# Where sixteen DRAM-to-DRAM copies of the window cache stand in SyncE's queue, in a two-layer hybrid decoder step

## The chip, the cores and the metric

The kernel runs on one core of a Trainium2 chip. The metric is device time in microseconds (us) of one execution; lower is better. Times of the kernel before are three timed runs and their median; the trace comes from one further execution under the hardware profiler.

## What is computed

One inference step of a decoder, two layers deep, for a prompt of 512 tokens and 8 sample sequences of one token each. Every layer normalizes its input, multiplies by `w_in`, runs a convolution branch and a sparse-attention branch, multiplies by `w_out`, normalizes and adds the residual. Beside the two activations the step returns updated caches. One of them is the point here: the window cache of the samples, 512 rows of keys and values per sequence, shifted up by one row with the new token's row put last.

```
win_rows = jnp.stack([kw, vw], axis=2)
win_ext = jnp.concatenate([pad_rows, win_buf, win_rows], axis=1)
win_new = win_ext[:, win_ext.shape[1] - n_keep:]
```

So for each layer and each of 8 sequences 511 of 512 old rows are copied from the input `cache_win` to the output one row higher: 16 copies of 1022 KB, from DRAM to DRAM. Nothing in the kernel reads them again.

## The kernel before

Each layer runs through four stages. `phase_a1` multiplies the normalized input by most of `w_in`, while the generator `compress` gathers pages of the cache (tile `G`, GpSimd), transposes them (tile `T`, VectorE), splits each into a high and a low part (`th`, `tl`) and multiplies by the compression weights (`w1f`, split into `w1h` and `w1l`). `phase_a2` does the rest of `w_in` and the attention of the samples. `phase_b` does the attention of the prompt, head by head, with column blocks of the `w_out` product as filler. `phase_c` finishes the `w_out` product and, in layer 0, starts the compression of layer 1.

A matrix product (`gemm`) loads 512 KB of weights into `wf` (two buffers, line 332), splits them into `wh` (ScalarE, line 374) and `wl` (VectorE or GpSimd, line 375), and multiplies three times per tile: `wh` by the high part of the input (350), `wh` by the low part (351), `wl` by the high part (352), into PSUM tile `g`.

In `phase_b`, `heads()` goes over four key/value heads. Each loads its keys twice into `kk` (one tile for the selected, one for the window branch, line 1436; split into `kh` and `kl`) and its values into `vnat`, and then over four query heads: a head loads its rotated query into `qq` (three buffers, two DMAs, line 1456), makes `qs` of it, and runs `stage1` (scores, softmax in `smx`) and `stage2` (transposes, product with values into `po`) for both branches. After every second head the gate `zt` (one buffer) is loaded and multiplied in on GpSimd (1422). Ahead of the heads stands the softmax of the compressed blocks, tile `sct`, whose exponential is line 1305.

All plain DMAs are issued by SyncE (SP), in the order of its program; indirect gathers are issued by GpSimd. The order of each engine's program is not the order of the Python code: a scheduler simulates the kernel when it is built and lets each engine take, by priority, what its simulation finds ready. Loads of weights are marked high priority. A copy of the window cache reads only an input and writes only an output, so it is ready at any moment. `tc.issue_after(ins)` adds an order edge: what the block issues on that engine stands behind `ins` in its program.

Of the kernel before, what the change touches and what calls it, by code (L numbers as in the profile page):

```python
# [372 lines left out]
def split(g, dst_h, dst_l, src, eng=None):  # L373
    g.nc.scalar.activation(dst_h, src, AF.Copy)  # L374
    return (eng or g.nc.vector).tensor_tensor(dst_l, src, dst_h.bitcast(F32), op=ALU.subtract)  # L375
# [382 lines left out]
def shift_window(g, l, s):  # L758
    n = 4 * 511
    row = 2 * NKV * HD  # L760
    at = (l * NS + s) * WIN * row
    g.nc.sync.dma_start(
        bass.AP(g.wins_o.tensor, at, [[n, 128], [1, n]]),
        bass.AP(g.a["cache_win"].tensor, at + row, [[n, 128], [1, n]]),
    )
# [498 lines left out]
def phase_b(g, l, mix):  # L1264
    nc, tc, K, ident = g.nc, g.tc, g.K, g.ident
    q_d, qr_d, kr_d, kvn_d, z_d = g.q_d[l], g.qr_d[l], g.kr_d[l], g.kvn_d[l], g.z_d[l]
    gnat = g.gnat
    with ExitStack() as sb:
# [6 lines left out]
        for kv in range(4):  # L1275
            pst = mi.tile([128, 512], F32, tag="t", bufs=PS_T, name="psc_t")
            for t2 in range(2):
                qt = pool.tile([128, SEQ], F32, tag="qq", name="qu", bufs=3)
                nc.sync.dma_start(qt, q_d[2 * kv + t2, :, 0:SEQ])
                for par in range(2):  # L1280
                    gg = 2 * t2 + par
# [147 lines left out]
        def heads():  # L1429
            units = []  # L1430
            for kv in range(4):
                kh_, kl_, vs_ = [], [], []
                for ty in range(2):
                    kk = pool.tile([128, SEQ], F32, tag="kk", name="kk")
                    for hh in range(2):
                        nc.sync.dma_start(
                            kk[64 * hh:64 * hh + 64], kr_d[2 * ty + kv // 2, 64 * (kv % 2):64 * (kv % 2) + 64, 0:SEQ]
                        )
                    kh2 = pool.tile([128, SEQ], F32R, tag=f"kh{ty}", name="kh2")
                    kl2 = pool.tile([128, SEQ], F32R, tag=f"kl{ty}", name="kl2")  # L1440
                    split(g, kh2, kl2, kk, nc.gpsimd)
                    kh_.append(kh2)
                    kl_.append(kl2)
                    vn_ = pool.tile([128, 4, 64], F32, tag="vnat", name="vnat")
                    c0 = (3 + 2 * ty) * 256 + kv * 64
                    nc.sync.dma_start(vn_, kvn_d[:, c0:c0 + 64].rearrange("(t p) f -> p t f", p=128))
                    v2 = pool.tile([128, 4, 128], F32R, tag=f"v2{ty}", name="v2")
                    split(g, v2[:, :, 0:64], v2[:, :, 64:128], vn_, nc.gpsimd)
                    vs_.append(v2)
                for s in (2 * kv, 2 * kv + 1):  # L1450
                    shift_window(g, l, s)
                for gg in range(4):
                    h = 4 * kv + gg
                    qq = pool.tile([128, SEQ], F32, tag="qq", name="qq", bufs=3)
                    for hh in range(2):
                        nc.sync.dma_start(
                            qq[64 * hh:64 * hh + 64], qr_d[h // 2, 64 * (h % 2):64 * (h % 2) + 64, 0:SEQ]
                        )
                    qs = pool.tile([128, SEQ], F32R, tag="qs", name="qs")
                    nc.scalar.activation(qs, qq, AF.Copy)  # L1460
                    nc.gpsimd.tensor_tensor(qs[64:128], qq[64:128], qs[64:128].bitcast(F32), op=ALU.subtract)
                    for ty in range(2):
                        units.append(stage1(h, ty, qs, kh_[ty], kl_[ty], vs_[ty]))
                        if len(units) > 1:
                            stage2(*units.pop(0))
            stage2(*units.pop(0))
# [9 lines left out]

        fill = gemm(g, _jobs(g.a["w_out"][l], 0, range(NPART), ks=(0, CT), width=128), mix, ev_part)
        heads()
        for _ in fill:
            pass  # L1480
# [190 lines left out]
```

## Time and profile before

| | before |
|---|---|
| timed runs | 3060.17, 3066.3, 3069.18 us |
| median | 3066.3 us |
| profiled execution: time, span | 3078.59 us, 3076.8 us |
| TensorE busy (share of the span) | 2707.9 us (88%) |
| VectorE | 2276.5 us (74%) |
| GpSimd | 1711.5 us (56%) |
| ScalarE | 1444.1 us (47%) |
| mean granted TensorE clock | 0.959 |
| bytes moved by DMA | 534.49 MB, mean 174 GB/s |

A busy share is a mean over stages with different limits; the section of rows below looks at stages. The profiled execution is 12.3 us longer than the median of the timed runs.

### The profile page before, as it was taken

What the parts mean: (1) busy time and instruction counts of PE and PEld (TensorE: products, weight loads), DVE (VectorE), ACT (ScalarE), POOL (GpSimd) and SP (SyncE); (2) the same over time, 40 slices, a digit from 0 to 9 for tenths busy, and PEclk for the clock granted to TensorE, in tenths of its full rate; (3) what the DMA queues carried; (4) which work ended last, traced back from release to release, by engine and by line L of the source; (5) the groups of instructions that cost most, each with busy time, mean ns of one, the idle gap of its engine ahead of it and who ended that gap; (6) DMA issues with size and microseconds to landing.
All of it is one profiled execution on the core that took longest, in us unless ns stands there. A gap on an engine that the chain in (4) does not pass through costs nothing. (4 is left out here: it accounts for less than half of the span.)

```text
span 3076.8 us, 53806 instructions
## 1 busy us (share of the span) xinstructions
PE 2707.9 (88%) x18984; PEld 2369.6 (77%) x18984; DVE 2276.5 (74%) x4432; ACT 1444.1 (47%) x3180; POOL 1711.5 (56%) x1610
## 2 busy tenths in 40 slices
PE   5498889989997998988988899899889899998896
PEld 4477778868786876867876688888878788887795
DVE  6479988877777643896999977897678765368746
ACT  4244344443333454785556544444333345468744
POOL 3376666655475654674656645565465565467502
PEclk8799999999998999999999999999999999999998
DMA  9876667755544645215777776675554464541154
GB/s 310 260 212 201 202 202 230 218 153 171 181 151 133 201 138 156 90 28 143 206 232 222 238 204 209 190 221 177 151 183 138 132 205 150 156 131 51 44 172 157
DMA packets 430318, 534.49 MB, mean 174 GB/s; under 512 B 68450, under 2 KB 357362, under 8 KB 429760
## 3 DMA queue, kind: packets, MB, share of 16 engines
q1 hardware_dynamic: 367328, 324.42, 35.4%
q0 software_dynamic: 62720, 206.63, 21.6%
q8 instruction: 149, 2.44, 0.3%
q14 instruction: 121, 0.99, 0.1%
HBM read 484.80 MB, written 64.75 MB: 179 GB/s over the span
## 5 line engine op out<-in xcount | busy, mean ns | idle before, releaser
L350 PE MATMUL g<-uh,wh 128*128 128x256 f32 (+1 forms) x3328 | 963.0, 292 | 74.8 <-ACT wh L374 60.1
L351 PE MATMUL g<-ul,wh 128*128 128x256 f32 (+1 forms) x3328 | 957.5, 290 | 0.0
L352 PE MATMUL g<-uh,wl 128*128 128x256 f32 (+1 forms) x3328 | 942.2, 291 | 11.3 <-DVE wl L375 11.3
L539 POOL DMA_INDIRECT G<-in_cache_kv_pages_dram,gix x512 | 543.5, 1062 | 355.0 <-DVE T L550 187.3
L350 PEld LDWEIGHTS g<-uh,wh 128*128 128x128 f32 x3328 | 644.0, 194 | 108.8 <-ACT wh L374 62.1
L375 DVE TENSOR_TENSOR wl<-wf,wh 128x512 fp32r<-128x512 f32 x565 | 429.0, 763 | 387.2 <-ACT wh L374 379.9
L1112 POOL DMA_INDIRECT G<-in_cache_kv_pages_dram,six x448 | 495.5, 1106 | 336.2 <-issue 113.9
L351 PEld LDWEIGHTS g<-ul,wh 128*128 128x128 f32 x3328 | 644.8, 194 | 22.9 <-issue 14.9
L352 PEld LDWEIGHTS g<-uh,wl 128*128 128x128 f32 x3328 | 633.6, 194 | 34.6 <-DVE wl L375 14.5
L374 ACT ACTIVATE wh<-wf 128x512 fp32r<-128x512 f32 x616 | 381.1, 625 | 462.1 <-PE g L351 250.2
L375 DVE TENSOR_TENSOR tl<-T,th 128x512 fp32r<-128x512 f32 x512 | 430.7, 861 | 98.3 <-ACT th L374 96.0
L374 ACT ACTIVATE th<-T 128x512 fp32r<-128x512 f32 x512 | 308.7, 624 | 312.4 <-DVE T L550 208.7
L550 DVE STREAM_TRANSPOSE T<-G 128x512 f32<-128x512 f32 x512 | 349.7, 695 | 22.0 <-DMA G<-in_cache_kv_pages_dram,gix 20.0
L887 DVE SCALAR_TENSOR_TENSOR c<-ap,cwt,c 128x512 f32<-128x512 f32 x480 | 339.4, 746 | 0.1
L579 PE MATMUL ca<-tl,w1h 128*128 128x512 f32 x512 | 218.5, 427 | 44.4 <-DVE tl L375 43.9
L578 PE MATMUL ca<-th,w1h 128*128 128x512 f32 x512 | 217.0, 424 | 24.0 <-ACT th L374 20.4
L375 POOL TENSOR_TENSOR w1l<-w1f,w1h 128x512 fp32r<-128x512 f32 x128 | 168.2, 1316 | 123.2 <-ACT w1h L374 96.3
L580 PE MATMUL ca<-th,w1l 128*128 128x512 f32 x512 | 209.2, 409 | 0.0
L1376 POOL TENSOR_TENSOR smx<-smx,su 128x256 f32<-128x256 f32 (+2 forms) x192 | 154.3, 830 | 84.0 <-DVE su L1370 63.6
L374 ACT ACTIVATE w1h<-w1f 128x512 fp32r<-128x512 f32 x128 | 79.5, 624 | 168.1 <-DMA w1f<-in_cmp_w_dram 85.7
L350 PE MATMUL g<-mha,wh 128*128 128x256 f32 (+1 forms) x512 | 144.7, 291 | 15.1 <-DVE zg L1513 8.3
L1368 ACT ACTIVATE smx<-smx,nm 128x128 f32<-128x128 f32 (+3 forms) x256 | 140.7, 552 | 35.9 <-DVE nm L1364 32.7
(1179 smaller groups left out, 5210.3 us busy)
## 6 DMA issues: line engine op xcount, KB each, us to landing
wf<-in_w_in_dram SPq DMA_DIRECT2D x220, 512.0 KB
wf<-in_w_out_dram SPq DMA_DIRECT2D x88, 512.0 KB
w1f<-in_cmp_w_dram SPq DMA_DIRECT2D x512, 64.0 KB
out_dram<-in_cache_win_dram SPq DMA_DIRECT2D x16, 1022.0 KB
G<-in_cache_kv_pages_dram,gix POOLq DMA_INDIRECT x512
wk<-in_cache_win_dram SPq DMA_DIRECT2D x16, 512.0 KB
qq<-qr_d SPq DMA_DIRECT2D x64, 128.0 KB
G<-in_cache_kv_pages_dram,six POOLq DMA_INDIRECT x448
```

Of the source, the lines that this page charges most:

```text
L350: nc.tensor.matmul(ps[m][h], lh, xh[:, sl], start=first, stop=False)
L351: nc.tensor.matmul(ps[m][h], lh, xl[:, sl], start=False, stop=False)
L352: pe = nc.tensor.matmul(ps[m][h], ll, xh[:, sl], start=False, stop=last)
L374: g.nc.scalar.activation(dst_h, src, AF.Copy)
L375: return (eng or g.nc.vector).tensor_tensor(dst_l, src, dst_h.bitcast(F32), op=ALU.subtract)
L539: nc.gpsimd.indirect_dma_start(out=G[:, i, :], out_offset=None, in_=g.pages, in_offset=bass.IndirectOffsetOnAxis(ap=g.gix[:, un * 4 + hs:u ...
L550: nc.vector.transpose(T.rearrange("p a b c -> p a (b c)"), G[:, :, c * 256:(c + 1) * 256])
L578: nc.tensor.matmul(acc[c], w1h[:, c, e], hi, start=f, stop=False)
L579: nc.tensor.matmul(acc[c], w1h[:, c, e], lo, start=False, stop=False)
L580: nc.tensor.matmul(acc[c], w1l[:, c, e], hi, start=False, stop=la)
L887: ce.scalar_tensor_tensor(c[:, :SEQ], ap[:, j:j + SEQ], cwt[:, i, j:j + 1], c[:, :SEQ], op0=ALU.mult, op1=ALU.add)
L1112: nc.gpsimd.indirect_dma_start(out=G[:np_, h, :], out_offset=None, in_=g.pages64, in_offset=bass.IndirectOffsetOnAxis(ap=six[:np_, s * 4 + ...
```

## The change

The two copies of a key/value head, which stood ahead of its four query heads, are issued one each behind the second DMA of the query load of the odd heads, and an order edge holds them there in SP's program. Sizes, count and addresses stay the same: query head `h` odd carries the copy of sequence `h // 2`.

```
-                for s in (2 * kv, 2 * kv + 1):
-                    shift_window(g, l, s)
                 for gg in range(4):
                     h = 4 * kv + gg
                     qq = pool.tile([128, SEQ], F32, tag="qq", name="qq", bufs=3)
                     for hh in range(2):
-                        nc.sync.dma_start(
+                        ld = nc.sync.dma_start(
                             qq[64 * hh:64 * hh + 64], qr_d[h // 2, 64 * (h % 2):64 * (h % 2) + 64, 0:SEQ]
                         )
+                    if gg % 2:
+                        with tc.issue_after(ld.ins):
+                            shift_window(g, l, h // 2)
```

How the built programs differ. At the start of the program, on SP, the kernel before has these rows between the first compression weights (`w1f`) and the third load of layer 0's `w_in` weights (`x_d` is the transposed input written back to DRAM; line 762 is the copy):

```order
L495 DMA w1f<-in_cmp_w_dram 32x4x128 x8
L762 DMA out_dram<-in_cache_win_dram 16x16352
L432 DMA x_d_79<-x_368 128x2x520
L762 DMA out_dram<-in_cache_win_dram 16x16352
L432 DMA x_d_79<-x_400 128x2x520
L762 DMA out_dram<-in_cache_win_dram 16x16352 x14
L332 DMA wf<-in_w_in_dram 128x4x256 x2
```

The changed kernel has these rows at the same place on SP:

```order
L495 DMA w1f<-in_cmp_w_dram 32x4x128 x4
L432 DMA x_d_79<-x_368 128x2x520
L495 DMA w1f<-in_cmp_w_dram 32x4x128 x2
L432 DMA x_d_79<-x_400 128x2x520
L776 DMA gb<-in_gate_b_dram 48x1
L332 DMA wf<-in_w_in_dram 128x4x256
L780 DMA wg<-in_w_in_dram 128x16x48
L332 DMA wf<-in_w_in_dram 128x4x256
L495 DMA w1f<-in_cmp_w_dram 32x4x128 x8
```

All 16 copies, of both layers, have left this place, and the weight loads follow the write-back directly.

In `phase_b` of layer 1, on SP, where the first heads' queries and keys are loaded, the kernel before has:

```order
L1456 DMA qq<-qr_d_84 64x512 x2
L1436 DMA kk<-kr_d_86 64x512 x2
L332 DMA wf<-in_w_out_dram 128x8x128
L1456 DMA qq<-qr_d_84 64x512 x2
L1436 DMA kk<-kr_d_86 64x512 x2
L1456 DMA qq<-qr_d_84 64x512 x2
L1436 DMA kk<-kr_d_86 64x512 x2
```

and the changed kernel (its query load is line 1454):

```order
L1454 DMA qq<-qr_d_84 64x512 x2
L1436 DMA kk<-kr_d_86 64x512 x2
L332 DMA wf<-in_w_out_dram 128x8x128
L762 DMA out_dram<-in_cache_win_dram 16x16352
L1454 DMA qq<-qr_d_84 64x512
L1436 DMA kk<-kr_d_86 64x512 x2
L1454 DMA qq<-qr_d_84 64x512 x3
L762 DMA out_dram<-in_cache_win_dram 16x16352
L1436 DMA kk<-kr_d_86 64x512
L332 DMA wf<-in_w_out_dram 128x8x128
L1436 DMA kk<-kr_d_86 64x512
```

The first copy of the layer now stands right ahead of the second key load of the first key/value head, the second copy right ahead of a key load of the next one; the other six stand farther along. Layer 0 has the same pattern.

At that place ScalarE's program before takes both key tiles of the first head (`kh_30235`, `kh_30247`) and then the exponential of line 1305:

```order
L374 ACTIVATE kh_30235<-kk 128x512
L1474 ACTIVATE pe<-g_32872 128x256
L374 ACTIVATE wh<-wf 128x512
L374 ACTIVATE kh_30247<-kk 128x512
L1305 ACT_TABLE_LOAD
L1305 ACTIVATE sct<-sct 128x512
L374 ACTIVATE wh<-wf 128x512
L1474 ACTIVATE pe<-g_32873 128x264
L374 ACTIVATE kh_30787<-kk 128x512
L374 ACTIVATE kh_30799<-kk 128x512
L374 ACTIVATE wh<-wf 128x512
L1368 ACTIVATE smx,su_30283<-smx,nm_30281 128x128
```

and in the changed kernel:

```order
L374 ACTIVATE kh_30235<-kk 128x512
L1475 ACTIVATE pe<-g_32872 128x256
L374 ACTIVATE wh<-wf 128x512
L1305 ACT_TABLE_LOAD
L1305 ACTIVATE sct<-sct 128x512
L374 ACTIVATE wh<-wf 128x512
L1475 ACTIVATE pe<-g_32873 128x264
L374 ACTIVATE kh_30247<-kk 128x512
L374 ACTIVATE wh<-wf 128x512
L1368 ACTIVATE smx,su_30281<-smx,nm_30279 128x128
```

The second key tile has moved behind the exponential, and both tiles of the next key/value head (`kh_30787`, `kh_30799`) behind the first head's softmax (1368).

## Rows read from the trace of the kernel before

**Rows 1.** The page: what DMA moved in 40 equal slices of the span.
```profile
GB/s 310 260 212 201 202 202 230 218 153 171 181 151 133 201 138 156 90 28 143 206 232 222 238 204 209 190 221 177 151 183 138 132 205 150 156 131 51 44 172 157
```

**Rows 2.** Windows: length, busy PE, PEld, DVE, ACT, POOL, clock, DMA share, GB/s.
```profile
47.00:65.00 18.00, 17.08 (x122) 14.93 (x120) 13.57 (x19) 6.25 (x12) 10.94 (x10) 1.00 1.00 356
65.00:116.00 51.00, 0.27 (x3) 0.11 (x1) 3.33 (x6) 2.60 (x5) 2.29 (x2) 0.54 0.91 306
70.00:110.00 40.00, 0.00 (x0) 0.00 (x0) 0.00 (x0) 0.00 (x0) 0.39 (x1) 0.50 0.96 327
116.00:200.00 84.00, 78.59 (x525) 68.15 (x526) 72.08 (x104) 39.80 (x70) 56.69 (x51) 0.95 0.73 218
200.00:400.00 200.00, 177.58 (x1178) 157.88 (x1177) 177.61 (x291) 81.64 (x142) 130.75 (x114) 0.98 0.68 205
```

**Rows 3.** Waits between 40 and 130 us: total, times, longest.
```profile
PE g L350 <- ACT wh L374: 50.7, 1, 50.7
DVE wl L375 <- ACT wh L374: 49.9, 3, 46.9
ACT wh L374 <- DMA wf<-in_w_in_dram: 47.3, 2, 47.0
POOL wl L375 <- ACT wh L374: 46.0, 1, 46.0
```

**Rows 4.** Timeline of SP from 49 us: start, duration, issue.
```profile
49.85 34.05 SPq L762 DMA_DIRECT2D out_dram<-in_cache_win_dram  x14
87.17 3.63 SPq L332 DMA_DIRECT2D wf<-in_w_in_dram  x2
93.74 23.17 SPq L495 DMA_DIRECT2D w1f<-in_cmp_w_dram  x8
```

**Rows 5.** DMA issues by line, count and size of each.
```profile
wf<-in_w_in_dram SPq DMA_DIRECT2D x220, 512.0 KB
...
w1f<-in_cmp_w_dram SPq DMA_DIRECT2D x512, 64.0 KB
out_dram<-in_cache_win_dram SPq DMA_DIRECT2D x16, 1022.0 KB
...
x_d<-x SPq DMA_DIRECT2D x8, 520.0 KB
```

**Rows 6.** Timeline of TensorE behind the idle stretch.
```profile
115.89 0.58 PE L350 MATMUL g<-uh,wh 128*128 128x256 f32 x1 [50.73 <-ACT wh L374]
...
119.96 0.42 PE L350 MATMUL g<-uh,wh 128*128 128x256 f32 x1
120.17 0.41 PE L351 MATMUL g<-ul,wh 128*128 128x256 f32 x1
...
120.55 0.28 PE L350 MATMUL g<-uh,wh 128*128 128x264 f32 x1
120.67 0.28 PE L351 MATMUL g<-ul,wh 128*128 128x264 f32 x1
```

**Rows 7.** Windows of the prompt attention, layer 0; columns as in rows 2.
```profile
1196.00:1300.00 104.00, 99.07 (x723) 88.80 (x722) 71.62 (x205) 68.07 (x187) 67.77 (x66) 1.00 0.44 131
1300.00:1410.00 110.00, 96.63 (x571) 75.94 (x570) 98.04 (x314) 88.74 (x251) 78.82 (x87) 0.98 0.10 28
```

**Rows 8.** ScalarE's waits for key loads, layer 0, 1180 to 1420 us.
```profile
ACT kh L374 <- DMA kk<-kr_d: 7.5, 2, 5.1
```

**Rows 9.** Timeline of ScalarE at the first heads of layer 1.
```profile
2707.51 0.63 ACT L374 ACTIVATE kh<-kk 128x512 fp32r<-128x512 f32 x1 [0.95 <-DMA kk<-kr_d]
...
2715.02 0.63 ACT L374 ACTIVATE kh<-kk 128x512 fp32r<-128x512 f32 x1 [3.62 <-DMA kk<-kr_d]
...
2717.07 0.40 ACT L1368 ACTIVATE smx<-smx,nm 128x128 f32<-128x128 f32 x1 [0.90 <-DVE nm L1364]
```

**Rows 10.** A gate load on SP and its first use on GpSimd, layer 0.
```profile
1292.75 0.34 SPq L1421 DMA_DIRECT2D zt<-z_d  x1
1319.71 1.27 POOL L1422 TENSOR_TENSOR om<-om,zt 128x512 f32<-128x512 f32 x1
```

## Prediction

> **What bounds the kernel now.** I read the page first: DMA moves most in the first slice (310 GB/s) and least in slice 18 and in slices 37 and 38 (28, 51 and 44 GB/s) [rows 1]. Those are the later halves of the two prompt attentions; the first is where the copies run now. So I cut the start into windows. Between 65 and 116 us TensorE works 0.27 us of 51, no other engine over 3.4, and from 70 to 110 there is nothing but 0.39 us of GpSimd, while DMA runs at 0.96 of its engines and 327 GB/s [rows 2]. Before and after that hole TensorE is at about nine tenths and VectorE between 0.75 and 0.9 of the time [rows 2]: this stage is bound by compute, except there.
>
> The waits tell who ended the hole: TensorE waited 50.7 us for `wh` (ScalarE), VectorE 46.9 and GpSimd 46.0 for the same, and ScalarE 47.0 us for the DMA of `wf` [rows 3]. All four stand behind one weight load. SP's timeline tells why it was late: from 49.85 to 83.9 us SP issued 14 copies of the window cache in one run, and only at 87.17 two `wf` loads, which then stood behind the copies that had not yet moved [rows 4]. ScalarE's wait for them ends about 115.2 (TensorE restarts at 115.89 [rows 6]), so the load took some 28 us, though 512 KB [rows 5] at the measured 327 GB/s is 1.6 us. The size check closes: 16 copies of 1022 KB [rows 5] are 16 x 1.0465 = 16.74 MB, and at 327 GB/s [rows 2] that is 51.2 us, 3.2 us each. The hole is 50.7 us. Nothing in the kernel needs the copies.
>
> **The change, part by part.** *Removed from the start:* 16 issues on SP and 51.2 us of all DMA engines. In the built program `x_d` writes, `wf` and `w1f` now follow each other directly there. The saving is the idle time before TensorE's first late matmul, 50.7 us [rows 6]. If the pace of the stage were set by VectorE or GpSimd it would be 46.9 or 46.0 [rows 3]; I take TensorE's, since its restart is the last of the four. Saving: **-50.7** (bounds -46.0 to -50.7).
>
> *The clock after the hole.* The granted clock is 0.50 through it [rows 2], the level of 1.2 GHz, and TensorE restarts there: its matmuls begin 0.21 us apart (119.96, 120.17) and 0.12 apart from 120.55 on [rows 6], where it is back at 2.4 GHz. From 115.89 to 120.4 that is 4.5 us of work that takes 4.5 x 0.12 / 0.21 = 2.5 at full clock: **-2.0** if TensorE is the limit there, nothing if VectorE is. I take -2.0, since between 116 and 200 us TensorE is busier (78.59) than VectorE (72.08) [rows 2].
>
> *What the hole did for free.* While engines stood still, the loads behind the copies came in too: two `wf` (1.05 MB), eight `w1f` of 64 KB (0.52 MB), one write of `x_d` (0.53 MB) [rows 5], and two gathers (0.26 MB each, 128 rows of 512 floats in the code). In the new start these some 2.6 MB share the engines with work: at 327 GB/s at most 8.0 us. DMA runs at 0.73 of its engines in 116 to 200 us and 0.68 after [rows 2], so about a quarter is spare and much of the 2.6 MB slips in. **+4** (bounds 0 to 8).
>
> *Added to the prompt attention:* eight copies per layer, 3.2 us each of all DMA engines, 25.6 us per layer. There is room: DMA is at 0.44 and 0.10 in its two halves [rows 7]. What matters is what stands behind a copy on SP's queue. Six of eight copies stand where the next loads are far ahead of their use: a gate load is issued at 1292.75 and used at 1319.71 [rows 10], 27 us, and `qq` has three buffers, so a query is loaded two heads ahead; with 16 heads in the 214 us of both windows [rows 7] that is some 27 us. 3.2 us late costs nothing there; if that cover were gone, each would cost up to 3.2. The first two copies of each layer are different: key loads stand right behind them, and ScalarE waits for keys already now, 7.5 us in layer 0 [rows 8] and 0.95 + 3.62 in layer 1 [rows 9]. Fully exposed, 4 x 3.2 = 12.8 us. But ScalarE's program has been moved to suit. Before, the second key tile stood ahead of the exponential (it was taken at 2707.51 [rows 9]), and a late key held the whole softmax of the compressed blocks up. Now it stands behind the exponential, and the next use of ScalarE for a head's softmax is at 2717.07 [rows 9]: a tile that lands at 2710.7 instead of 2707.5 is in time. The second copy is ahead of the next head's two tiles, the later of which was taken at 2715.02 after a wait of 3.62 us [rows 9]; they now stand behind the first head's softmax. TensorE is covered by filler in that half (99.07 of 104 us busy [rows 7]). I take a quarter of the bound: **+3** (bounds 0 to 12.8).
>
> *The scheduler's reshuffle.* Orders change in small ways all along, since the simulated clock moved; the proportion of compression matmuls to weight matmuls along TensorE's program stays the same to a few instructions. I count it 0, with some 5 us either way.
>
> A rule of the Trainium skill that speaks against the change is in "DMA: Bandwidth & Descriptors", section "Queues, rings and completion order": SP owns one ring per DMA engine and each engine consumes it in ring order, so a load behind a copy waits for all of it. By that rule, the trace agrees: the `wf` loads issued at 87.17 took 28 us. By the fit for one DMA in the Trainium skill's "DMA: Bandwidth & Descriptors" (section "Anatomy of one DMA — SWDGE (gpsimd) path"), 2.0 us plus bytes at 436 GB/s, an estimate of one copy is 4.4 us and the exposed bound would be 17.6 us instead of 12.8; the trace's 3.2 us per copy is used.
>
> **Sum** against the profiled execution: 3078.6 - 50.7 - 2.0 + 4 + 3 = 3032.9 us, 45.7 less. That execution stood 0.4% above the median of the timed runs (3078.59 to 3066.3), so for the median: 3066.3 x 3032.9 / 3078.6 = **3021 us**, -1.5%. With every bound at its best, -52.7, it is 3014; at its worst, -46.0 + 8 + 12.8 = -25.2, it is 3041.
>
> **Rivals.**
>
> *The start becomes bound by DMA.* Without the copies the first 150 us must still carry what the first 200 carry now. For the 84 us behind the hole that is 84 us x 218 GB/s = 18.3 MB and the 2.6 MB, 20.9 MB or 249 GB/s, against 205 in the steady stretch [rows 2]. Speaks against it: 327 and 356 GB/s were reached [rows 2]. If a third of the hole comes back as shorter waits for `w1f` and `wf`, +17 us: 3038. Chance 0.12.
>
> *Every copy holds up its head.* The place is the queue behind each copy; the price is 3.2 us for the wait and, if TensorE falls to 1.2 GHz in it and restarts as it did at 115.89, 2.0 more, 5.2 us each. 16 x 5.2 = 83 against 52.7 saved: 30 us longer, 3096. It decides when the mean cost per copy exceeds 52.7 / 16 = 3.3 us. For it: ScalarE does wait for key loads already [rows 8, 9]. Against: the 27 us of lead [rows 10] and the idle DMA [rows 7]. Between nothing and this lies the case that it eats the gain exactly (3.3 us each): no change. Chance 0.03 slower, 0.02 same.
>
> *The hole is not the copies'.* If `wf` were late for another reason (SP also spent 23.17 us on eight `w1f` issues just behind it [rows 4]), the hole would stay and the time be 3066 + 3, about the same. Against it: those issues come after the `wf` loads, and 51.2 us of copies fit 50.7 of hole. Chance 0.02.
>
> **Numbers.** The forecast (3004 to 3034) has 0.80, the DMA-bound start 0.12, the others 0.07, and 0.01 is left for a gain beyond 3004. Faster or slower by 0.3% (9 us) is what a measurement of this kernel can tell from no change. Faster: 0.80 + 0.12 + 0.01 = 0.93; same 0.04; slower 0.03. The range goes from 3004 (the best bound, 3014, with the reshuffle and the spread of the timed runs, 9 us, taken off) to 3043 (the worst bound and the second rival).
>
> **What would show it.** Right: in the new trace TensorE has no hole over some 8 us between 50 and 130 us, DMA there shows no stretch at 0.96 with idle engines, the granted clock does not fall to 0.50 at 70 us, the prompt attention of layer 0 begins some 49 us sooner than 1196, and DMA in its later half rises from 28 GB/s to about 66 (the last four copies, 4.2 MB, in 110 us). The spans of both prompt attentions stay within 3 us of before. Wrong: ScalarE's waits for `kk` and `qq` grow by 3 us a copy and the attentions lengthen by 10 us or more each; or new waits for `w1f` and `wf` of over 15 us in the first 200 us; or the hole stays.

## The result, and the profile after

| | before | after |
|---|---|---|
| median of the timed runs | 3064.59 us | 3024.98 us |
| lowest to highest | 3060.17 to 3069.18 (4 runs) | 3020.52 to 3029.22 (4 runs) |
| ratio, 95% interval | | 0.987, 0.9849 to 0.9891 |
| profiled execution: time, span | 3078.59, 3076.8 us | 3029.22, 3027.1 us |
| mean granted TensorE clock | 0.959 | 0.963 |

The change makes the kernel 39.6 us faster, 1.3%. The forecast was 3021 us, within 3004 to 3043. One later group of runs (e9 to e11 below) took 4.6% longer as a whole, the kernel before included (3205.03 us); of that group only comparisons within it are used.

First the hole. The windows of the start in the profile after (columns as in [rows 2]: length, busy time of TensorE, its weight loads, VectorE, ScalarE and GpSimd, granted clock, DMA share, GB/s):

```profile
47.00:65.00 18.00, 17.90 (x131) 15.94 (x131) 16.30 (x23) 8.07 (x14) 11.40 (x11) 0.99 0.81 208
65.00:116.00 51.00, 46.59 (x321) 39.90 (x319) 41.34 (x63) 24.91 (x44) 35.42 (x33) 1.00 0.75 225
116.00:150.00 34.00, 30.46 (x200) 25.51 (x201) 29.10 (x44) 15.64 (x29) 24.20 (x22) 1.00 0.71 210
```

Where TensorE worked 0.27 of 51 us before [rows 2] it now works 46.59, at the full clock, and DMA is at 0.75 of its engines instead of 0.91. The two largest waits between 40 and 130 us, after (total, times, longest):

```profile
ACT w1h L374 <- DMA w1f<-in_cmp_w_dram: 18.9, 5, 4.4
POOL G L539 <- DVE T L550: 15.4, 6, 9.1
```

No wait for `wf` is left near the top, and none like the four of 46 to 51 us in [rows 3]. ScalarE's waits for `w1f` in this stretch are new, 18.9 us together, but no single one is over 4.4 us, and TensorE's 46.59 of 51 us show that little of them reaches it. SP's timeline after (start, duration, issue), the place where 14 copies stood in [rows 4]:

```profile
52.31 0.39 SPq L332 DMA_DIRECT2D wf<-in_w_in_dram  x1
52.75 0.50 SPq L780 DMA_DIRECT2D wg<-in_w_in_dram  x1
55.63 1.27 SPq L332 DMA_DIRECT2D wf<-in_w_in_dram  x1
57.01 5.05 SPq L495 DMA_DIRECT2D w1f<-in_cmp_w_dram  x8
```

The two `wf` loads that were issued from 87.17 us on, the first of which took 28 us, now go out at 52 and 56 us. The copies of layer 0 have gone to its prompt attention, where SP issues them one at a time (first and last of eight):

```profile
1155.75 0.59 SPq L762 DMA_DIRECT2D out_dram<-in_cache_win_dram  x1
...
1306.82 0.58 SPq L762 DMA_DIRECT2D out_dram<-in_cache_win_dram  x1
```

The windows of that attention after, shifted by 52 us against [rows 7], and the page's line of DMA traffic, to be set beside [rows 1]:

```profile
1144.00:1248.00 104.00, 97.47 (x703) 86.50 (x702) 69.52 (x196) 66.39 (x178) 65.35 (x63) 1.00 0.58 179
1248.00:1358.00 110.00, 96.67 (x562) 77.61 (x562) 98.06 (x316) 88.74 (x254) 77.28 (x85) 0.95 0.18 54
```

```profile
GB/s 264 228 210 213 210 210 236 194 119 186 151 160 174 132 148 199 118 36 188 213 237 217 236 208 202 208 228 144 161 181 151 128 214 146 153 186 97 61 161 155
```

TensorE's busy time in the two halves is 97.47 and 96.67 us (99.07 and 96.63 before), and DMA has gone from 131 to 179 and from 28 to 54 GB/s. Five copies are issued in the first half and three in the second: 5 x 1.0465 MB in 104 us are 50 GB/s, 3 x 1.0465 in 110 us are 29, which is the growth. (The prediction had counted four in the second half, hence its 66 GB/s.) ScalarE's waits for loads in this attention (1127 to 1370 us), beside [rows 8]:

```profile
ACT v L374 <- DMA vnat<-kvn_d: 4.8, 2, 4.2
ACT kh L374 <- DMA kk<-kr_d: 4.6, 4, 1.7
ACT qs L1461 <- DMA qq<-qr_d: 2.3, 1, 2.3
```

The waits for keys have become four short ones of 4.6 us together, less than the 7.5 before.

**Where the time went, by landmarks.** The profile of one tile gives the first and the last start of its instructions (line, engine, tiles, count: least/median/greatest duration in ns, first and last start in us). Five products serve as landmarks and cut the span: the first `psc_t` (scores against the compressed blocks, the beginning of the attention), the last `ps_s` of layer 0, the first `p_sum` from `acco` (column sum at the end of layer 0), the last `pkt` (transpose in the compression of layer 1, near the end of its first stage) and the last `psy` (end). Before, the first two rows read between 1100 and 1500 us:

```profile
L1282 PE MATMUL psc_t<-qu,kcp x32: 588/601/614, 1186.8 to 1204.7; 64*32 64x512 f32 x32
L1352 PE MATMUL ps_s<-kl,qs x128: 224/334/521, 1213.4 to 1399.3; 128*128 128x128 f32 x32, 128*128 128x256 f32 x32, 128*128 128x384 f32 x32, 128*128 128x512 f32 x32
L387 PE MATMUL p_sum<-acco,ones x8: 377/381/461, 1589.2 to 3049.6; 128*128 128x256 f32 x4, 128*128 128x264 f32 x4
L722 PE MATMUL pkt<-const,kf x64: 270/272/329, 127.4 to 2104.1; 128*128 128x128 f32 x64
L1551 PE MATMUL psy<-const,zg x64: 270/373/450, 3013.6 to 3068.3; 128*128 128x128 f32 x64
```

and after:

```profile
L1282 PE MATMUL psc_t<-qu,kcp x32: 589/602/682, 1136.2 to 1152.7; 64*32 64x512 f32 x32
L1352 PE MATMUL ps_s<-kl,qs x128: 273/332/628, 1160.7 to 1352.7; 128*128 128x128 f32 x32, 128*128 128x256 f32 x32, 128*128 128x384 f32 x32, 128*128 128x512 f32 x32
L387 PE MATMUL p_sum<-acco,ones x8: 377/380/462, 1546.4 to 2999.8; 128*128 128x256 f32 x4, 128*128 128x264 f32 x4
L722 PE MATMUL pkt<-const,kf x64: 270/272/329, 78.9 to 2057.8; 128*128 128x128 f32 x64
L1552 PE MATMUL psy<-const,zg x64: 270/374/449, 2964.4 to 3018.5; 128*128 128x128 f32 x64
```

Stretch by stretch, after minus before: up to layer 0's attention 1136.2 - 1186.8 = -50.6; that attention 216.5 against 212.5, +4.0; from there to the first `p_sum` 193.7 against 189.9, +3.8; layer 1's first stage 511.4 against 514.9, -3.5; the rest, which holds layer 1's attention with the other eight copies, 960.7 against 964.2, -3.5. The sum is -49.8 = 3018.5 - 3068.3.

### The profile page after: what moved, and what is told of

Read it like the earlier page. It is cut to its first block, busy times and chain, and to the rows that moved or that the text cites. A ratio compares the mean times of both kernels' runs of the same rounds, so it can differ in the third digit from the quotient of the medians.

```text
span 3027.1 us, 53793 instructions
## 1 busy us (share of the span) xinstructions
PE 2716.8 (90%) x18984; PEld 2378.5 (79%) x18984; DVE 2278.1 (75%) x4432; ACT 1446.6 (48%) x3180; POOL 1713.4 (57%) x1610
## 5 line engine op out<-in xcount | busy, mean ns | idle before, releaser
L350 PE MATMUL g<-uh,wh 128*128 128x256 f32 (+1 forms) x3328 | 962.5, 292 | 18.6 <-ACT wh L374 8.6
L351 PEld LDWEIGHTS g<-ul,wh 128*128 128x128 f32 x3328 | 645.0, 194 | 23.2 <-issue 15.3
L550 DVE STREAM_TRANSPOSE T<-G 128x512 f32<-128x512 f32 x512 | 349.8, 695 | 24.9 <-DMA G<-in_cache_kv_pages_dram,gix 23.2
L579 PE MATMUL ca<-tl,w1h 128*128 128x512 f32 x512 | 217.9, 426 | 43.4 <-DVE tl L375 42.9
```

The costliest lines, as they stand in the source:

```text
L350: nc.tensor.matmul(ps[m][h], lh, xh[:, sl], start=first, stop=False)
L351: nc.tensor.matmul(ps[m][h], lh, xl[:, sl], start=False, stop=False)
L550: nc.vector.transpose(T.rearrange("p a b c -> p a (b c)"), G[:, :, c * 256:(c + 1) * 256])
L579: nc.tensor.matmul(acc[c], w1h[:, c, e], lo, start=False, stop=False)
```

## The experiments

The theory: the hole was the copies' run ahead of the weight loads in one queue, and beside other work the copies are almost free. Rivals: the copies cost their bandwidth wherever engines work; and the two early copies of a layer, or all, hold up the heads behind them. The diffs are against the changed kernel; each ratio is to the kernel before, timed in the same group of runs (e1 to e4, e5 to e8, e9 to e11). The built programs of two kernels can be compared line by line, and that turned out to matter: when a copy moves, the scheduler may write another order for stages far from it.

**No copies (e1).** The window cache is not written; the rest is as it was.

```
-                    if gg % 2:
-                        with tc.issue_after(ld.ins):
-                            shift_window(g, l, h // 2)
```

> Leaves the 16 copies of the window cache out altogether (most rows of that output are then not written). Theory 1 (copies are nearly free inside the prompt attention, about 3 us in all): 3022 us, within 4 us of the changed kernel's 3025, and the first 130 us look like the changed kernel's. Theory 2 (copies still cost what the measured gain lacks to the 52 us saved at the start, some 10 us): 3014 us, and the prompt attention of layer 0 is some 5 us shorter than in the changed kernel.

Measured 2997.12 us (2994.27 to 2997.96, 5 runs; before 3068.51 beside it): ratio 0.9767 [0.9751, 0.9783]. So the change, at 0.987, leaves 1.0% on the table. Both expected times (3022 and 3014) were too long: what the changed kernel loses is more than the +3 us which the prediction had for the copies in the attentions, and the next runs look for it.

**The copies of layer 1 back at the start (e2).**

```
+                if l == 1:
+                    for s in (2 * kv, 2 * kv + 1):
+                        shift_window(g, l, s)
...
-                    if gg % 2:
+                    if gg % 2 and l == 0:
```

> Layer 0's 8 copies stay behind the query loads, layer 1's 8 are free again and stand at the start (3 and 5 in a run, around one write of x_d). Theory 1 (each copy in the run at the start holds the weight loads for its whole transfer of 3.2 us): TensorE idles about 25 us near 65 us, and the time is 3025 + 25 = 3050 us. Rival (weight buffers absorb a shorter run): hole under 10 us, 3030 to 3035 us.

Measured 3042.98 us (3033.59 to 3044.45), ratio 0.9909 [0.9886, 0.9932]. SP's timeline, a window and the waits (40 to 130 us) of its profile:

```profile
48.01 1.89 SPq L762 DMA_DIRECT2D out_dram<-in_cache_win_dram  x3
50.00 1.32 SPq L432 DMA_DIRECT2D x_d<-x  x2
51.37 6.76 SPq L762 DMA_DIRECT2D out_dram<-in_cache_win_dram  x5
61.12 0.38 SPq L332 DMA_DIRECT2D wf<-in_w_in_dram  x1
```

```profile
65.00:116.00 51.00, 27.82 (x187) 24.99 (x188) 27.99 (x39) 16.14 (x28) 18.40 (x17) 0.77 0.86 271
```

```profile
PE g L350 <- ACT wh L374: 23.2, 1, 23.2
ACT wh L374 <- DMA wf<-in_w_in_dram: 20.0, 2, 19.5
```

Eight copies ahead of the `wf` load make a hole of 23.2 us, sixteen made 50.7 [rows 3], none makes none (e1). The hole grows about in proportion to the copies that stand ahead of the load; with e8 below, where the same copies stand apart, that settles its cause. The time is 7 us below the expected 3050.

**Copies behind the late heads (e3).** One behind each query load of heads 8 to 15.

```
-                    if gg % 2:
+                    if h >= 8:
...
-                            shift_window(g, l, h // 2)
+                            shift_window(g, l, h - 8)
```

> All 8 copies of a layer behind the query loads of heads 8 to 15, one each, so none stands ahead of the first key loads. Theory 1 (the two early copies cost next to nothing, ScalarE's order covers them): 3025 us, within 4. Theory 2 (the early copies are what the attention of layer 0 lost): 3018 to 3020 us, and the time from the first score matmul to the first head's sum in layer 0 shrinks by 4 us.

Measured 2996.79 us (2993.97 to 3000.45, 5 runs), ratio 0.977 [0.9753, 0.9787]. It equals the copy-free kernel, and the built programs of TensorE, VectorE, ScalarE and GpSimd are the same in both, instruction for instruction: sixteen copies of 1022 KB cost nothing here that these runs can tell. Both expected times (3025, and 3018 to 3020) were too long again. This version beats both kernels. Its landmarks:

```profile
L1282 PE MATMUL psc_t<-qu,kcp x32: 588/601/614, 1126.8 to 1143.1; 64*32 64x512 f32 x32
L1352 PE MATMUL ps_s<-kl,qs x128: 273/332/522, 1152.0 to 1334.5; 128*128 128x128 f32 x32, 128*128 128x256 f32 x32, 128*128 128x384 f32 x32, 128*128 128x512 f32 x32
L387 PE MATMUL p_sum<-acco,ones x8: 378/382/491, 1527.5 to 2965.0; 128*128 128x256 f32 x4, 128*128 128x264 f32 x4
L722 PE MATMUL pkt<-const,kf x64: 270/273/329, 80.0 to 2024.3; 128*128 128x128 f32 x64
L1552 PE MATMUL psy<-const,zg x64: 270/332/449, 2929.5 to 2983.6; 128*128 128x128 f32 x64
```

Against the changed kernel: -9.4 us up to layer 0's attention, -8.8 in it (207.7 against 216.5), -0.7 to the first `p_sum`, -14.6 in layer 1's first stage (496.8 against 511.4), -1.4 in the rest: 34.9 between the two profiles, 28 between the medians. The largest piece lies in a stage in which neither kernel has a copy.

**All eight behind head 1 (e4).**

```
-                    if gg % 2:
+                    if h == 1:
...
-                            shift_window(g, l, h // 2)
+                            for s in range(8):
+                                shift_window(g, l, s)
```

> All 8 copies of a layer in a run behind the second head's query load. Queue theory (a load behind copies on SP's queue waits for all of them; 8 x 3.2 = 25.6 us per layer): key loads of the first two key/value heads come some 20 us late, ScalarE waits for them, and the time is 3045 to 3070 us. Bandwidth theory (DMA is idle there, so a transfer is free wherever it stands): 3025 us, within 5.

Measured 3031.54 us (3020.04 to 3035.18), ratio 0.9886 [0.9866, 0.9906]. Layer 0's attention is the longest of all, 221.2 us (1125.9 to 1347.1), but no hole appears, and ScalarE waits in it 1.9 us for keys and 2.9 us for queries, not the 20 us of the queue theory. The scheduler set two key loads between the copies and wrote an order of its own, so this is no clean test of the queue.

**Behind heads 0 to 7 (e5), and behind heads 3, 5, 7, 9, 11, 13, 15, 15 (e6).** The first keeps the copies early but has, behind layer 0's attention, the late-heads version's order; the second lets the first heads go and has there the changed kernel's order.

```
-                    if gg % 2:
-                        with tc.issue_after(ld.ins):
-                            shift_window(g, l, h // 2)
+                    for s in range(8):
+                        if list(range(0,8))[s] == h:
+                            with tc.issue_after(ld.ins):
+                                shift_window(g, l, s)
```

(e6 has `[3,5,7,9,11,13,15,15]` for the list.)

> Copies one each behind the query loads of heads 0 to 7, sooner and denser than in the change. Behind layer 0's attention its built program has, row for row, the order of the late-heads kernel (2997 us), not that of the changed kernel (3025). Order theory (the 28 us between those two come from the order that the scheduler gave the stages behind layer 0's attention, not from where the copies move): 2997 us plus at most 8 for the attentions, so under 3006. Copy theory (early copies hold up the first heads, and that is the 28 us): 3025 us or more.

> Copies behind the query loads of heads 3, 5, 7, 9, 11, 13 and two behind 15: the change without its first copy per layer. Behind layer 0's attention the built program has, row for row, the order of the changed kernel. Order theory: 3025 us, within 5. Copy theory (the first copy, ahead of the first keys, is what costs): 3010 us or less.

Measured: e5 3001.91 us (2999.47 to 3002.14; before 3064.46), ratio 0.9799 [0.9776, 0.9821]; e6 3009.48 us (3001.36 to 3016.4), ratio 0.982 [0.9796, 0.9844]. Neither pure theory gives both: e5 came out as the order theory expected (under 3006), e6 as the copy theory did (3010 or less). Early copies with the late-heads version's order lose little against it, 5 us between the medians (3001.91 to 2996.79), some 9 by the ratios (0.9799 to 0.977). The changed kernel's order without the first copy, at 0.982, is below the 0.987 of the change, but the change timed again (e9 below) has 0.9834 with an interval that overlaps, so a gain from that copy is not shown.

**Layer 0 late, layer 1 odd heads (e7).**

```
-                    if gg % 2:
+                    if (h >= 8) if l == 0 else gg % 2:
...
-                            shift_window(g, l, h // 2)
+                            shift_window(g, l, h - 8 if l == 0 else h // 2)
```

> Layer 0 as in the late-heads kernel (heads 8 to 15), layer 1 as in the change (odd heads). Its order is that of the late-heads kernel up to layer 1's attention, so all that differs there is layer 1's attention. Order theory: 2997 us, plus at most 4 for layer 1's copies. Copy theory (each early attention costs half of the 28 us): 3011 us.

Measured 3001.33 us (2995.11 to 3007.42), ratio 0.9803 [0.9777, 0.9828]; as the order theory expected (2997 to 3001), and not to be told from the late-heads version.

**Copies in the first stage, but one per weight load (e8).** From the ninth weight load on, each is followed by one copy, until all 16 are out.

```
+    g.n_ld, g.copies = 0, [(l, s) for l in range(DEPTH) for s in range(NS)]
...
+            g.n_ld += 1
+            if g.n_ld > 8 and g.copies:
+                with tc.issue_after(g.dma_mark.ins):
+                    shift_window(g, *g.copies.pop(0))
...
-                    if gg % 2:
-                        with tc.issue_after(ld.ins):
-                            shift_window(g, l, h // 2)
```

> All 16 copies back in the first stage, but one each behind a weight load from the ninth on, instead of 16 in a run. Its order from layer 1 on is that of the changed kernel, so it is compared with 3025 us. Clump theory (the hole came from 16 copies in a run on one queue; DMA has a quarter to spare in this stage, 0.73 of its engines busy): no hole, small waits, 3025 to 3035 us. Bandwidth theory (the stage needs its DMA, so 51 us of transfers cost most of 51 us wherever they stand in it): 3055 to 3070 us.

Measured 3003.59 us (3001.05 to 3007.27, 4 runs), ratio 0.9808 [0.9781, 0.9835]. The copies' issues (least/median/greatest duration in ns, first and last start in us), a window of its start and one over the whole stretch of the copies:

```profile
L767 SPq DMA_DIRECT2D out_dram<-in_cache_win_dram x16: 515/521/684, 108.5 to 280.3; - x16
```

```profile
65.00:116.00 51.00, 46.85 (x324) 40.44 (x322) 43.02 (x62) 23.44 (x42) 35.62 (x34) 1.00 0.78 240
108.00:280.00 172.00, 157.68 (x1068) 139.77 (x1067) 152.05 (x246) 72.83 (x126) 111.94 (x100) 0.98 0.90 300
```

The second window in the profile after, which has no copy there:

```profile
108.00:280.00 172.00, 156.40 (x1060) 137.48 (x1059) 155.45 (x247) 73.84 (x129) 116.97 (x104) 1.00 0.72 211
```

All sixteen are issued between 108 and 280 us, in the stage that the change cleared. DMA moves 300 GB/s there instead of 211, and TensorE works 157.68 of 172 us, as without them (156.40). So it was never the bandwidth of the first stage: 16.7 MB fit into it if they are spread, and cost 51 us if they stand in a run. The time is below both expected ranges, since this version reaches layer 0's attention sooner than any other (table below).

**The changed kernel, a mixed version and the late heads side by side (e9 to e11).** So far the changed kernel had been timed apart from the others. e9 is the changed kernel and e11 the late-heads version (e3), both unaltered. e10 has layer 0 as the change and layer 1 late; its program is the changed kernel's word for word until layer 1's attention.

```
-                    if gg % 2:
+                    if (h >= 8) if l == 1 else gg % 2:
...
-                            shift_window(g, l, h // 2)
+                            shift_window(g, l, h - 8 if l == 1 else h // 2)
```

> The changed kernel once more, timed beside the two others of this group on one chip, because so far it was timed apart from the late-heads version, and its profiled execution stood 7 to 10 us behind the copy-free one at the first score product of layer 0's compressed branch, where both have run the same instructions and no copy has been issued. Theory 'place and order': its 28 us to the late-heads version are about 10 of early copies in layer 0's attention and 12 to 17 of the scheduler's order in layer 1's first stage: it measures 3018 to 3030 and the gap stays 22 to 33 us. Rival 'occasion': part of the gap is only that they were timed on different occasions: it measures 3005 to 3015 and the gap shrinks below 18 us.

> Layer 0's copies as in the change (odd heads), layer 1's behind the query loads of heads 8 to 15. The program is the changed kernel's word for word until layer 1's attention. Theory 'place and order': layer 1's places cost nothing, so it equals the changed kernel timed beside it within 5 us (3018 to 3030). Rival 'first heads of layer 1 pay too': it is 8 us or more faster than the changed kernel timed beside it. With the version that has layer 0 late and layer 1 odd (3001) this makes a two by two table of the places.

> The late-heads version again, beside the changed kernel on the same chip. Theory 'place and order': 2994 to 3001 as before, 22 to 33 us below the changed kernel. Rival 'occasion': the two stand within 18 us of each other.

Measured, beside 3205.03 us for the kernel before (11 runs): the change 3155.36, ratio 0.9834 [0.9807, 0.9862]; layer 0 odd, layer 1 late 3157.18, 0.9847 [0.9817, 0.9877]; late heads 3117.09, 0.9734 [0.9702, 0.9767]. The absolute times lie above the expected ones, as does that of the kernel before beside them. The gap between the change and the late heads is larger than expected, 38.3 us (22 to 33 expected), so the rival "occasion" falls. Where layer 1's copies stand makes no difference that these runs can tell (3157.18 against 3155.36, and e7 against e3). What decides is where layer 0's copies stand, and more through the order that the scheduler then writes than through the copies themselves: in e5 they stand early and the order is that of the late heads, and little is lost. That is an argument from several versions; no run changes the order alone.

**The stretches of all profiles**, from the same five landmarks as above (us; each from one profile):

| | to layer 0's attention | that attention | to `p_sum` | layer 1, first stage | rest |
|---|---|---|---|---|---|
| before | 1186.8 | 212.5 | 189.9 | 514.9 | 964.2 |
| after | 1136.2 | 216.5 | 193.7 | 511.4 | 960.7 |
| e1, no copies | 1128.7 | 209.4 | 191.0 | 496.7 | 961.4 |
| e2, layer 1 at the start | 1161.8 | 206.5 | 195.2 | 509.2 | 961.0 |
| e3, late heads | 1126.8 | 207.7 | 193.0 | 496.8 | 959.3 |
| e4, clump | 1125.9 | 221.2 | 197.3 | 504.4 | 961.1 |
| e5, heads 0 to 7 | 1127.6 | 218.1 | 192.3 | 498.5 | 955.1 |
| e6, from head 3 | 1127.9 | 210.1 | 192.3 | 516.0 | 959.3 |
| e7, layer 0 late | 1127.6 | 207.8 | 192.6 | 493.8 | 964.8 |
| e8, spread in the first stage | 1119.1 | 213.8 | 189.9 | 513.4 | 957.8 |
| e9, the change again | 1189.3 | 221.5 | 195.6 | 521.2 | 1026.4 |
| e10, layer 0 odd, layer 1 late | 1180.8 | 216.5 | 195.1 | 514.7 | 1024.9 |
| e11, late heads again | 1186.0 | 207.8 | 190.9 | 499.1 | 1016.9 |

The rows of e9 to e11 compare with one another only.

Layer 1's first stage has no copy in any of the kernels. TensorE's built program there is one and the same in after, e6, e9 and e10, and nearly the same in before and e8 (all but some 100 to 150 of 2960 matmuls in the same order): 511.4 to 521.2 us. It is another, common one in e1, e3, e5, e7 and e11: 493.8 to 499.1. The two sets do not overlap, wherever the copies stand; e2 and e4 have orders of their own and lie between. The last `pkt` stands 29 matmuls earlier in the second order (of 18460), so a part of the difference is work that comes behind the landmark; the last two columns together leave that out. From the first `p_sum` to the end before, after, e6 and e8 take 1471.2 to 1479.1 us, e1, e3, e5 and e7 1453.6 to 1458.6: 13 to 25 us apart. The medians show less: e6 and e5 are 8 us apart (3009.48 to 3001.91), and e6's profile is the slowest of its five runs (3016.4).

The whole stage as one window in the profile after, and 100 us of it, picked because the two orders differ much there:

```profile
1546.00:2058.00 512.00, 453.38 (x3031) 406.71 (x3031) 444.48 (x758) 252.17 (x494) 291.18 (x269) 0.96 0.72 217
```

```profile
1660.00:1760.00 100.00, 81.36 (x486) 71.63 (x485) 91.78 (x169) 51.98 (x102) 65.25 (x61) 0.93 0.78 235
```

and in the late-heads version:

```profile
1527.00:2024.00 497.00, 443.02 (x3007) 394.91 (x3006) 430.46 (x749) 245.03 (x485) 285.79 (x263) 0.98 0.73 220
```

```profile
1641.00:1741.00 100.00, 84.97 (x549) 74.12 (x548) 98.86 (x182) 52.59 (x104) 63.70 (x61) 1.00 0.81 245
```

Of the 15 us, 10.4 are busy time of TensorE (453.38 against 443.02; 24 of 3031 records fewer, at the mean of 0.15 us some 4 us of it) and 4.6 idle time; the granted clock is 0.96 against 0.98. In the 100 us the late-heads version runs 549 matmuls at a clock of 1.00 and the changed kernel 486 at 0.93. The clock of the whole stage goes with the order in every profile: 0.95 to 0.96 in the six of the first, 0.97 to 0.98 in the five of the second. Two of TensorE's waits in that stage tell how the orders differ. After:

```profile
PE ca L579 <- DVE tl L375: 18.6, 15, 3.8
PE ca L578 <- ACT th L374: 9.9, 11, 2.6
```

late heads:

```profile
PE ca L578 <- ACT th L374: 17.3, 13, 3.3
PE ca L579 <- DVE tl L375: 7.3, 13, 1.4
```

In one order the compression's products wait mostly for VectorE's low part `tl` (18.6 to 21.8 us in its six profiles), in the other for ScalarE's high part `th` (`tl` 6.7 to 11.4 us in its five); in these two profiles both waits together are 28.5 and 24.6 us. That the rest comes from the clock is a reading of these windows, not shown by an experiment.

## Why the prediction was right, and what in it was not

**The hole, -50.7.** Right, with its cause: without a run of copies there is no hole (e1, e3, e8), with half the copies it is 23.2 us (e2). The saving to the start of layer 0's attention is 50.6 us in the profile after, and the prediction's first three terms sum to -50.7 - 2.0 + 4 = -48.7. That match is partly luck. One more landmark, the first `pkt` from `ksx` (a transpose near the end of the first stage), splits the stretch; before, then after:

```profile
L737 PE MATMUL pkt<-const,ksx x2: 271/273/275, 552.2 to 2109.5; 128*96 128x128 f32 x2
L737 PE MATMUL pkt<-const,ksx x2: 272/294/315, 493.5 to 2063.4; 128*96 128x128 f32 x2
```

At that landmark the change is already 58.7 us ahead. Six other profiles of the first two groups (e1, e3 to e7) run the same program on TensorE up to layer 0's attention, and are 57.3 to 61.7 us ahead there. So the first stage gained some 8 us more than the idle time, of which the prediction had 2, for the clock. From the landmark to the attention the change's own profile took 642.7 us, against 634.6 before and 633.8 to 635.6 in the six, and lost the 8 us again. What the rest of the extra gain is stays open: TensorE's order in the first stage is not that of before, and the one profile of before lies 14.0 us above its median.

**The clock, -2.0.** The granted clock stays at 0.99 to 1.00 where it fell to 0.50 [rows 2]; the 2 us by themselves are too small to be seen apart.

**What the hole did for free, +4.** Not seen. The six profiles reach layer 0's attention at 1125.9 to 1128.7 us, 58.1 to 60.9 sooner than before, which is more than the best bound (-52.7). The changed kernel's own profile stands 8 to 10 us behind them, with no copy yet issued; among e9 to e11, same program again, the three differ by 8.5 us (1180.8 to 1189.3). So one profile of this stretch is good to some 8 us, and neither the 4 nor its sign could have been read from one; the six together speak for 0, the bound at the other end, or better. The prediction's own sign for a DMA-bound start, new waits for `w1f` of over 15 us in the first 200, is there (29.8 us in eight pieces, 9.5 in three before) and yet meant nothing: e1, without any copies, has 28.0 us of them, and e8 added 16.7 MB to that stage and reached the attention at 1119.1.

**The attentions, +3.** The sum is small, as forecast: +4.0 in layer 0 (212.5 to 216.5), and in layer 1, cut the same way, -3.2 (217.9 to 214.7); both just miss the "within 3 us". The mechanism, late keys, is not what the +4.0 shows: ScalarE's waits for keys shrank (7.5 to 4.6 us) and those for queries stayed (2.2 and 2.3). The rival that every copy holds up its head (3096) falls.

**The reshuffle, 0 within 5.** For the change itself it held from layer 1 on: before and after have nearly the same TensorE order in layer 1's first stage, and the stretches there and behind differ by 3.5 us each. It is less sure for layer 0's first stage, where the two orders differ: from the first `pkt` from `kf` to the first from `ksx` before takes 424.8 us and after 414.6, the six profiles of its program 412.3 to 416.7, and e8, with a third order and all copies in it, 400.6. As a bound on what the scheduler's order can do in this kernel it was too narrow. From the first `p_sum` to the end the two orders are 13 to 25 us apart, and within layer 0's attention orders differ as well: before and e8, one program there and no copies in it, take 212.5 and 213.8 us, e1, e3 and e7, another common program, 207.7 to 209.4. The change stayed in the order of before in layer 1, so its term there was near 0; the late-heads version, in the other, is at 2997, below the predicted range.

**From the profile to the median.** The profile fell by 49.4 us (3078.59 to 3029.22), the sum of terms by 45.7, the medians by 39.6 in the first timing and by 49.7 (3205.03 to 3155.36) in the last group. The profile before lies 14.0 us above its median and the one after 4.2, which is the difference between 49.4 and 39.6. The forecast's closeness to the median (3021 against 3025) therefore rests on terms that missed in both directions as well as on the hole, which was right.

**Left open.** Layer 0's attention is 7 to 12 us above the copy-free length with early copies (after 216.5, e9 221.5, e5 218.1, e4 221.2 against 209.4). How much of that is the early copies' queueing and how much the order that the scheduler writes around them is not shown; e2 has its copies at the same heads as the change and takes 206.5, and some 2 us are eight more matmuls that fall between the landmarks. Nor is it shown which single inversion makes the order of layer 1's first stage faster, and what sets the spread of 8 us between executions of one program.

## What to carry to other kernels

A scheduler may take a bulk transfer that depends on nothing as early as it can, and if the transfer shares a queue with loads it can make a hole as long as itself: look for a stretch in which DMA is full and every engine idle, and check that bytes over rate equals the hole. Break the run rather than seek an empty stage: one copy behind each load did nearly as well in a busy stage (3004 us, ratio 0.9808) as in the attentions' late heads (2997, 0.977), where DMA had most to spare. The late heads are better than the change beside it (e11 and e9); the spread copies were not timed beside it. Where a scheduler writes the order, compare the built programs of variants before explaining a difference, since a moved instruction can go with 13 us and more in a stage far from it. And look at a second profile before reading a term of a few microseconds from one.

## What the runs showed of the hardware

While copies from DRAM to DRAM, 1022 KB each, ran in a row and the engines stood idle, DMA moved 327 GB/s [rows 2]. One per weight load, they ran beside engines that did not slow down, with 300 GB/s in total: TensorE ran 1068 matmuls from 108 to 280 us in e8, 1060 in the profile after without them. A 512 KB load behind 14 of them in one queue took some 28 us [rows 4, 6]. One program reached the same landmark up to 10.3 us apart in seven profiles (1125.9 to 1136.2 us) and 8.5 in three others (1180.8 to 1189.3). The late one of the seven lost its time behind the first stage, where its granted clock was lower: 0.95 from 493 to 998 us, against 0.97 from 492 to 988 in e3. What lowered it is not shown. In the three profiles of e9 to e11 TensorE stood still for 97 to 100 us in all, in some 140 short pieces, with nothing to wait for that the profile shows; the other ten profiles have no such waits of TensorE.
